# Moving the half-width set to place two, and the seven-product sets to places 3, 5 and 6

## The chip, the core and the metric

The kernel runs on one core of a Trainium2 chip. The metric is the device time of one launch in microseconds (us). TensorE does the matmuls (PE in the profile, with its weight loads as PEld), VectorE is DVE, ScalarE is ACT, GpSimd is POOL, and SyncE (SP) issues most transfers from HBM. Each of these engines works through its own instructions strictly in the order in which the built program has them, and waits where an operand is not there yet.

## The reference

A decoder trunk of four layers on 256 tokens of width 1024, all in float32. Each layer is: half a step of a SwiGLU feed-forward net, a token mixer, and half a step of a second feed-forward net. So there are eight feed-forward nets (FFNs), and the change touches only these:

```
def swiglu_ffn(x, w_gate_up, w_down):            # w_gate_up 1024 x 5632, w_down 2816 x 1024
    gate, up = jnp.split(x @ w_gate_up, 2, axis=-1)
    return (jax.nn.silu(gate) * up) @ w_down

x = x + 0.5 * rms_norm(swiglu_ffn(rms_norm(x, g[0]), ffn_w_gate_up[i, 0], ffn_w_down[i, 0]), g[1])
...                                              # the mixer
x = x + 0.5 * rms_norm(swiglu_ffn(rms_norm(x, g[4]), ffn_w_gate_up[i, 1], ffn_w_down[i, 1]), g[5])
```

## The kernel before, in words

**Precision.** Every float32 operand is split into a rounded part `hi` (written by ACT, L312) and the rest `lo` (written by DVE, L313). A product is three matmuls: hi·hi, hi·lo, lo·hi. Weights come from HBM as tiles of 128x1024 (512 KB), called units here. A unit is loaded into one of 5 `raw` buffers, split into one of 10 `hi`/`lo` buffer pairs (the ring, `RING = 10`), and used by PE. `pump` splits units ahead of their use, in the order of one list (`plan`), up to nine units ahead of the one that PE has finished with; `slot` is called after each unit, says that its buffers are free, issues one outstanding quad load and splits up to two units.

**An FFN.** The 2816 columns of the inner width are 22 blocks of 128. They are worked in six sets, each at a place in the order: `WIDTH` gives the blocks of each, five with 4 and one with 2. A full set makes 512 gate and 512 up columns for two tiles of 128 tokens. There are three ways to do a set:

- *The first set* and the one at place 5 are plain: eight units (g0 to g3, u0 to u3), each with 12 matmuls of 128x512.
- *The half-width set* (`e`, two blocks) puts 256 gate and 256 up columns in one tile: four units of 12 matmuls.
- *The seven-product sets* (function `seven`, the places in `SEVEN`) treat the set as a 2x2 block product (two token tiles, two halves of the 1024 inputs, gate and up columns) and do it with seven block products instead of eight. Each product (operations 0 to 6) is two split units of 6 matmuls, 84 matmuls in all against 96. The price is on the other engines. The weights come as four *quads* (tiles of 128x2x1024, two halves each, eight loads of 512 KB on SP), held in buffers that all FFNs share (`mgh`, `mgl`, `rows`) and one of the FFN's own (`q22`). They are added to each other in place: `gather` on POOL's queue adds one quad to another by DMA (L271, halves 0 and 1 of the fourth quad onto the second, later the sum onto the third), and DVE adds in place ahead of operation 2 (L285) and subtracts ahead of operation 4 (L288). All 14 splits then read the quads, so a split can wait for a gather. On the output side ACT copies an accumulator aside while PE goes on (`snap`, L632: after operations 0, 2 and 3), and DVE combines copies and accumulators (L644 after operation 1, L655 after 4, L661 after 5, L666 and L667 after 6).

**Down units.** One unit D of the down projection (12 matmuls for both token tiles) can be used once its block has been transposed. `FILL` says how many D units follow each part of a set; the last eight of the 22 are held back and done first for token tile 0, then for tile 1, so that the norm of tile 0 runs beside the second pass. A finished set is transposed (`turned`, L565 on PE, then splits on ACT and DVE) in the middle of the next one, the last set after the second of the eight held units.

**What sets the order.** The Python order of the calls fixes which unit is split and loaded when; a scheduler then places instructions on each engine's queue. PE, DVE, ACT, POOL and SP then run their queues in that order.

**Quad loads before.** `new_quad` makes the eight loads of a set outstanding. It is called at the start of the FFN for the set at place 2, and at the start of the set ahead for those at places 4 and 6.

Of the kernel before, what the change touches and what calls it, by code (L numbers as in the profile page):

```python
# [52 lines left out]
N_OUT = {0: 8, 1: 4, 2: 8}  # L53


WIDTH = (4, 4, 2, 4, 4, 4)
SETS = len(WIDTH)
FIRST = tuple(sum(WIDTH[:s]) for s in range(SETS))
SEVEN = (1, 3, 5)
FILL = {1: (2, 2), 2: (2,), 3: (2, 0), 4: (1, 1), 5: (2, 2)}  # L60
QUADS = 8


def ffn_chunks(l, f):
# [8 lines left out]
    for s in range(SETS):  # L73
        if s in SEVEN:
            for ops, n in zip(((0, 1, 2), (3, 4, 5, 6)), FILL[s]):
                order += [("S", l, f, s, op, h) for op in ops for h in range(2)]
                fill(n)
            continue
        for c, n in zip(("e",) if WIDTH[s] == 2 else ("g", "u"), FILL.get(s, (0, 0))):
            order += [(c, l, f, s, i) for i in range(4)]  # L80
# [125 lines left out]
class Trunk:  # L206
    def __init__(self, ctx, tc, io):
        self.ctx, self.tc, self.nc, self.io = ctx, tc, tc.nc, io
        pool = lambda name, bufs=1, **kw: ctx.enter_context(tc.tile_pool(name=name, bufs=bufs, **kw))
        self.const = pool("const")  # L210
        self.wp = pool("wp")
        self.main = pool("main")
        self.small = pool("small", 4)
        self.ps = pool("ps", space=bass.MemoryType.PSUM)
        self.dram = pool("dram", space=bass.MemoryType.DRAM)
        self.plan = plan()
        self.offs = {}
        o = 0
        for key in load_order():
            a, b = unit_shape(key)  # L220
            self.offs[key] = o
            o += P * a * b
        self.raw_order = [key for key in self.plan if key[0] != "S"]
        self.loaded = self.split_n = self.taken = self.released = 0
        self.raws = deque()
        self.ready = deque()
        self.bg = deque()
        self.xf = {}
        self.quad = None
        self.quad_loads = deque()  # L230

    def rot(self, *shape):
        t = self.ps.tile([P, 512], F32, tag="rot", name="rot", bufs=4)
# [17 lines left out]
        self.raws.append((t, a * b))  # L251
        self.loaded += 1

    def new_quad(self, fp, l, f, s):
        self.quad = [None] * 4
        self.quad_pool = fp
        self.quad_set = (l, f, s)
        self.quad_loads = deque(quads(l, f, s))

# [31 lines left out]
    def split_next(self):  # L291
        key = self.plan[self.split_n]
        hi = self.wp.tile([P, 1024], F32R, tag="hi", name="hi", bufs=RING)
        lo = self.wp.tile([P, 1024], F32R, tag="lo", name="lo", bufs=RING)
        if key[0] == "S":
            for _ in range(self.quads_for(key)):
                self.load_quad()
            self.split(hi, lo, self.operand(*key[4:]))
        else:
            t, n = self.raws.popleft()  # L300
            self.split(hi[:, :n], lo[:, :n], t[:, :n])
            self.load_next()
        self.ready.append((hi, lo))
        self.split_n += 1
# [232 lines left out]
    def ffn(self, l, f, post_next, pre_next, last=False):  # L537
        nc, tc = self.nc, self.tc
        with tc.tile_pool(name=f"ffn{l}{f}", bufs=1, reuse_waits="tile") as fp:
# [16 lines left out]
            def turn_set(s, t):  # L556
                if t == 0:
                    if WIDTH[s] == 2:
                        hs[s] = tuple(fp.tile([P, 2, SEQ], F32R, tag=n, name=n) for n in ("eh", "el"))
                    else:  # L560
                        hs[s] = tuple(fp.tile([P, 4, SEQ], F32R, tag=n, name=n, bufs=2) for n in ("hh", "hl"))
                n = WIDTH[s]
                ps = self.rot()
# [7 lines left out]
            def first_set():  # L571
                T[0] = [tile_T(), tile_T()]
                held = [self.take("g", l, f, 0, i) for i in range(4)]
                for t in range(2):
                    g = self.rot()
                    for i in range(4):
                        pair(held[i], g, i, t)
                        self.slot(t)
                    silu(T[0][t], g)
                    u = self.rot()  # L580
                    if t == 0:
                        held.extend(self.take("u", l, f, 0, i) for i in range(4))
                    for i in range(4):
                        pair(held[4 + i], u, i, t)
                        self.slot(t)
                        if t == 0 and i == 2:
                            self.trans(1, keep=self.keep)
                    nc.vector.tensor_tensor(out=T[0][t], in0=T[0][t], in1=u, op=ALU.mult)
# [80 lines left out]
                product(s, 6, c, False, c12)  # L669
                fill(FILL[s][1])  # L670

            self.new_quad(fp, l, f, 1)
            first_set()
            left = sums()
            gn = {"pre": None}
# [36 lines left out]

            for s in range(1, SETS):
                T[s] = [tile_T(), tile_T()]
                if s + 1 in SEVEN:
                    self.new_quad(fp, l, f, s + 1)
                if s in SEVEN:
                    seven(s)
                    if s == max(SEVEN):
                        self.bg.append(gains)  # L720
                    if s == max(SEVEN) and (l, f) == (0, 0):
                        self.bg.extend(self.setup2())
# [5 lines left out]
                after = lambda s=s: turned(s - 1)  # L728
                if WIDTH[s] == 2:
                    ps = half("e", s, after, 2)  # L730
# [617 lines left out]
```

## Time and profile before

| | |
|---|---|
| runs, median (lowest to highest of 3) | 1889.15 us (1886.43 to 1889.77) |
| the profiled execution, its own time | 1888.2 us |
| its span | 1886.4 us |
| PE, DVE, ACT, POOL busy | 98%, 81%, 60%, 8% of the span |
| granted TensorE clock, mean | 0.996 |
| splits: from raw tiles, from quads | 451 and 336 on ACT, as many on DVE |
| gathers on POOL | 96, twelve to an FFN |

The profiled execution is 0.95 us under the median. A matmul is shown as 0.39 us though the next one starts 0.227 us after it: they are pipelined, and PE's busy share says little about waits. Waits on PE are read from the idle time with its releaser, and from distances between starts.

### The profile page before, as it was taken

Reading aid. Unit: us, or ns where it says so; the run is one execution under the profiler, and the core shown is the slowest. Engines: PE = TensorE matmul, PEld = TensorE weight load, DVE = VectorE, ACT = ScalarE, POOL = GpSimd, SP = SyncE. Lnnn points to the kernel's source line nnn. Section 1 sums busy time; section 2 is a strip of 40 time slices with the busy share of each in tenths; the row PEclk is TensorE's granted clock in tenths of the full one; section 3 lists DMA queues with packets and bytes.
Section 4 is the critical chain, followed back from the end, with each engine's and each line's share of the span. In section 5 each row is a group of like instructions: output and inputs, shape, how many; then the busy total and the mean of one; then the engine's idle time right before and its main releaser. Section 6 shows DMA issues by size and latency. Waiting matters only on the chain.

```text
span 1886.4 us, 25346 instructions
## 1 busy us (share of the span) xinstructions
PE 1842.0 (98%) x9310; PEld 1535.2 (81%) x9310; DVE 1537.1 (81%) x1868; ACT 1132.7 (60%) x1541; POOL 150.2 (8%) x211
## 2 busy tenths in 40 slices
PE   7999999999999999999999999999999999999998
PEld 5788887878788797778878889877788888987886
DVE  6888878987988768888789876879887988879884
ACT  5666656656665655656666666556665666656652
POOL 0000201000100100100010000010001000201000
PEclk9999999999999999999999999999999999999999
DMA  8886748776786662677668667358775786738862
GB/s 295 257 265 225 224 136 264 227 243 223 226 261 194 235 220 101 201 242 247 215 210 263 211 218 257 105 190 256 247 245 169 245 264 204 247 125 273 256 192 78
DMA packets 117692, 413.01 MB, mean 219 GB/s; under 512 B 13620, under 2 KB 18112, under 8 KB 117440
## 3 DMA queue, kind: packets, MB, share of 16 engines
q1 hardware_dynamic: 103568, 359.47, 54.2%
q0 software_dynamic: 14000, 51.92, 13.8%
q8 instruction: 73, 1.20, 0.3%
q14 instruction: 51, 0.42, 0.1%
HBM read 359.95 MB, written 1.06 MB: 191 GB/s over the span
## 4 chain that ended last, share of the span: by engine, by line
PE 41%; DVE 7%; DMA 3%; issue 2%; ACT 1%; POOL 1%; DVEq 0%; ACTq 0%; POOLq 0%
PE acc L696 12%; PE rot L624 9%; PE rot L337 5%; PE rot L339 5%; PE rot L338 5%; DVE lo L313 5%; PE acc L960 2%; DMA quad<-quad 2%; DMA quad<-in_w 1%; PE rot L565 1%; PE acc L880 1%; DVE quad L288 1%; PE rot L894 1%; PE rot L862 1%; ACT hi L312 0%
## 5 line engine op out<-in xcount | busy, mean ns | idle before, releaser
L313 DVE TENSOR_TENSOR lo<-raw,hi 128x1024 fp32r<-128x1024 f32 (+2 forms) x451 | 536.3, 1217 | 77.6 <-ACT hi L312 74.7
L312 ACT ACTIVATE hi<-raw 128x1024 fp32r<-128x1024 f32 (+2 forms) x451 | 463.2, 1051 | 198.3 <-DMA raw<-in_w 96.7
L312 ACT ACTIVATE hi<-quad 128x1024 fp32r<-128x1024 f32 x336 | 343.6, 1053 | 227.5 <-DVE quad L285 131.8
L313 DVE TENSOR_TENSOR lo<-quad,hi 128x1024 fp32r<-128x1024 f32 x336 | 397.5, 1219 | 20.7 <-ACT hi L312 19.9
L339 PE MATMUL rot<-hi,xtl 128*128 128x512 f32 (+3 forms) x816 | 312.8, 384 | 3.9 <-DVE xtl L313 3.9
L337 PE MATMUL rot<-hi,xth 128*128 128x512 f32 (+3 forms) x816 | 315.0, 386 | 0.4 <-ACT hi L312 0.4
L338 PE MATMUL rot<-lo,xth 128*128 128x512 f32 (+3 forms) x816 | 312.0, 382 | 0.3 <-DVE lo L313 0.3
L624 PE MATMUL rot<-hi,sums 128*128 128x512 f32 x768 | 255.1, 398 | 16.2 <-ACT snap L632 8.0
L696 PE MATMUL acc<-hi,hh 128*128 128x512 f32 x640 | 199.4, 391 | 0.0
L696 PE MATMUL acc<-lo,hh 128*128 128x512 f32 x640 | 198.9, 390 | 0.0
L696 PE MATMUL acc<-hi,hl 128*128 128x512 f32 x640 | 197.9, 390 | 0.0
L624 PEld LDWEIGHTS rot<-hi,sums 128*128 128x128 f32 x768 | 145.8, 190 | 52.9 <-ACT snap L632 12.3
L339 PEld LDWEIGHTS rot<-hi,xtl 128*128 128x128 f32 x816 | 153.7, 188 | 37.0 <-DVE xtl L313 8.3
L337 PEld LDWEIGHTS rot<-hi,xth 128*128 128x128 f32 x816 | 153.8, 189 | 29.2 <-ACT hi L312 1.0
L338 PEld LDWEIGHTS rot<-lo,xth 128*128 128x128 f32 x816 | 153.8, 188 | 29.2 <-DVE lo L313 0.5
L624 PE MATMUL rot<-lo,sums 128*128 128x512 f32 x384 | 151.2, 394 | 2.1 <-DVE lo L313 2.1
L271 POOL DMA_DIRECT2D quad<-quad x96 | 83.7, 897 | 837.6 <-DMA quad<-in_w 394.5
L696 PEld LDWEIGHTS acc<-hi,hl 128*128 128x128 f32 x640 | 119.6, 188 | 26.9 <-DVE hl L313 2.2
L696 PEld LDWEIGHTS acc<-lo,hh 128*128 128x128 f32 x640 | 119.9, 188 | 24.7
L696 PEld LDWEIGHTS acc<-hi,hh 128*128 128x128 f32 x640 | 119.7, 188 | 24.5
L624 PE MATMUL rot<-hi,xtl 128*128 128x512 f32 x288 | 112.1, 389 | 0.0
L624 PE MATMUL rot<-hi,xth 128*128 128x512 f32 x288 | 112.0, 389 | 0.0
(214 smaller groups left out, 2571.3 us busy)
## 6 DMA issues: line engine op xcount, KB each, us to landing
raw<-in_w SPq DMA_DIRECT2D x440, 512.0 KB, 4.8
quad<-in_w SPq DMA_DIRECT2D x192, 512.0 KB, 5.1
quad<-quad POOLq DMA_DIRECT2D x96, 512.0 KB, 4.7
gpre<-in_norm_g SPq DMA_DIRECT2D x8, 512.0 KB, 6.3
gpost<-in_norm_g SPq DMA_DIRECT2D x8, 512.0 KB, 3.4
memraw<-in_mem_t SPq DMA_DIRECT2D x32, 128.0 KB, 3.6
g<-in_norm_g SPq DMA_DIRECT2D x8, 512.0 KB, 6.7
raw<-in_w SPq DMA_DIRECT2D x8, 384.0 KB, 4.1
```

The costliest lines, as they stand in the source:

```text
L271: self.nc.gpsimd.dma_start(out=x, in_=y, accum_op=ALU.add)
L288: self.nc.vector.tensor_tensor(out=b11, in0=b11, in1=b22, op=ALU.subtract)
L312: self.nc.scalar.activation(out=hi, in_=src, func=AF.Copy)
L313: self.nc.vector.tensor_tensor(out=lo, in0=src, in1=hi.bitcast(F32), op=ALU.subtract)
L337: mm(out, a[0], b[0], start=start, stop=False)
L338: mm(out, a[0], b[1], start=False, stop=False)
L339: mm(out, a[1], b[0], start=False, stop=stop)
L565: nc.tensor.transpose(ps[:, k * P:(k + 1) * P], T[s][t][:, k * P:(k + 1) * P], self.ident)
L624: nc.tensor.matmul(ps, a[i], w[j][:, kk, :], start=fresh and h == kk == i == j == 0, stop=h == kk == i == 1, skip_group_check=True)
L696: mm(ys[t][:, n * 512:(n + 1) * 512], x, y[:, 0, n * 512:(n + 1) * 512], start=(j == 0 and x is a[0] and y is w[0]), stop=(j == NF - 1 and ...
L862: nc.tensor.transpose(ps[:, i * P:(i + 1) * P], blocks[b0 + i], self.ident)
L960: self.nc.tensor.matmul(o["y"][t][:, h * 512:(h + 1) * 512], x, y[:, 0, h * 512:(h + 1) * 512], start=(j == 0 and x is a[0] and y is w[0]) ...
```

## The change

Three tables and the time at which quad loads are made outstanding are changed. The half-width set goes from place 3 to place 2. The seven-product sets go from places 2, 4 and 6 to places 3, 5 and 6, and the plain set from place 5 to place 4, so that the last two sets are both seven-product sets and stand next to each other. The same units, matmuls and bytes are left; their order differs, and with it which columns belong to which set.

The D units between are dealt out anew. Fourteen are done ahead of the eight held ones, as before. A seven-product set had two in its middle (after operation 2) and now has one; six now stand between the seven-product sets at places 5 and 6, and none stands between the last product of place 6 and the held units, where there were two.

The quad loads of a set are now made outstanding in `split_next`, right after the second half of operation 6 of the seven-product set ahead is split (`new_quad` takes the next from `quad_wait`), and for the first of an FFN at the first set's up units, four slots later than before.

```
-WIDTH = (4, 4, 2, 4, 4, 4)
+WIDTH = (4, 2, 4, 4, 4, 4)
...
-SEVEN = (1, 3, 5)
-FILL = {1: (2, 2), 2: (2,), 3: (2, 0), 4: (1, 1), 5: (2, 2)}
+SEVEN = (2, 4, 5)
+FILL = {1: (2,), 2: (1, 1), 3: (1, 1), 4: (1, 6), 5: (1, 0)}
...
+        self.quad_wait = deque()
...
-    def new_quad(self, fp, l, f, s):
+    def new_quad(self):
+        self.quad = None
+        if not self.quad_wait:
+            return
+        self.quad_pool, l, f, s = self.quad_wait.popleft()
         self.quad = [None] * 4
-        self.quad_pool = fp
         self.quad_set = (l, f, s)
         self.quad_loads = deque(quads(l, f, s))
...
             self.split(hi, lo, self.operand(*key[4:]))
+            if key[4:] == (6, 1):
+                self.new_quad()
...
                     if t == 0:
+                        self.quad_wait.extend((fp, l, f, s) for s in SEVEN)
+                        self.new_quad()
                         held.extend(self.take("u", l, f, 0, i) for i in range(4))
...
-            self.new_quad(fp, l, f, 1)
             first_set()
...
-                if s + 1 in SEVEN:
-                    self.new_quad(fp, l, f, s + 1)
                 if s in SEVEN:
                     seven(s)
```

In the changed file the lines stand a little lower: the split is L318 and L319, the gather L275, the additions L289 and L292, the transposes L571, the products L632, the copy aside L640, the combinations L652, L663, L669, L674 and L675, and the D units L703.

**Gathers on POOL, layer 1, first FFN.** Each seven-product set has four: two add the fourth quad to the second, two add the sum that DVE makes of it to the third, and the last two cannot start before DVE has read what the first two made. Before, in the order of places 2, 4 and 6:

```order
L271 DMA quad_4298<-quad_4313 128x1024 x2
L271 DMA quad_4280<-quad_4261 128x1024 x2
L271 DMA quad_4808<-quad_4833 128x1024
L271 DMA quad_4751<-quad_4716 128x1024
L271 DMA quad_4808<-quad_4833 128x1024
L271 DMA quad_4751<-quad_4716 128x1024
L271 DMA quad_5188<-quad_5221 128x1024 x2
L271 DMA quad_5133<-quad_5096 128x1024 x2
```

Now, in the order of places 3, 5 and 6:

```order
L275 DMA quad_4344<-quad_4371 128x1024 x2
L275 DMA quad_4309<-quad_4294 128x1024 x2
L275 DMA quad_4741<-quad_4771 128x1024 x2
L275 DMA quad_4712<-quad_4683 128x1024 x2
L275 DMA quad_5181<-quad_5211 128x1024 x2
L275 DMA quad_5152<-quad_5123 128x1024 x2
```

At place 4 the second gather of the first kind stood behind a gather of the second kind. No set has that any more; it was so in six of the eight FFNs (all but the two of layer 0).

**PE at the end of the last set, layer 1, first FFN.** L624 is the last matmul of operation 6, `acc` the sum of the down projection, L565 the transposes of the last set's two token tiles. Before (the last row of operation 6 and ten of the 18 rows of D units; eight more follow, the last six of them of the first two held units, and then the transposes):

```order
L624 MATMUL rot_5441<-hi_5393,sums_4449 128x512
L696 MATMUL acc_4452<-hi_5409,hh_5139 128x512 x2
L696 MATMUL acc_4452<-lo_5410,hh_5139 128x512 x2
L696 MATMUL acc_4452<-hi_5409,hl_5140 128x512 x2
L696 MATMUL acc_4453<-hi_5409,hh_5139 128x512 x2
L696 MATMUL acc_4453<-lo_5410,hh_5139 128x512 x2
L696 MATMUL acc_4453<-hi_5409,hl_5140 128x512 x2
L696 MATMUL acc_4452<-hi_5421,hh_5139 128x512 x2
L696 MATMUL acc_4452<-lo_5422,hh_5139 128x512 x2
L696 MATMUL acc_4452<-hi_5421,hl_5140 128x512 x2
L696 MATMUL acc_4453<-hi_5421,hh_5139 128x512 x2
```

Now:

```order
L632 MATMUL rot_5477<-hi_5429,sums_4453 128x512
L703 MATMUL acc_4456<-hi_5445,hh_5395 128x512 x2
L703 MATMUL acc_4456<-lo_5446,hh_5395 128x512 x2
L703 MATMUL acc_4456<-hi_5445,hl_5396 128x512 x2
L703 MATMUL acc_4456<-hi_5457,hh_5395 128x512 x2
L703 MATMUL acc_4456<-lo_5458,hh_5395 128x512 x2
L703 MATMUL acc_4456<-hi_5457,hl_5396 128x512 x2
L703 MATMUL acc_4456<-hi_5471,hh_5395 128x512 x2
L703 MATMUL acc_4456<-lo_5472,hh_5395 128x512 x2
L571 MATMUL rot_5580<-ident_74,T_5344 128x128 x4
L571 MATMUL rot_5587<-ident_74,T_5345 128x128 x4
```

Between operation 6 and the transposes stood 36 matmuls (18 rows of two), and now stand 16. In the very last FFN it is 12.

**DVE at the same place.** From the split of operation 6's second half (from a quad) to the product that the transposes read (L667 before, L675 now), before:

```order
L313 TENSOR_TENSOR lo_5462<-raw_5272,hi_5461 128x1024
L655 TENSOR_TENSOR snap_5433<-rot_5441,snap_5433 128x512
L313 TENSOR_TENSOR lo_5474<-raw_5413,hi_5473 128x1024
L313 TENSOR_TENSOR lo_5489<-raw_5425,hi_5488 128x1024
L546 SCALAR_TENSOR_TENSOR T_5293<-T_5293,rot_5294 128x512
L313 TENSOR_TENSOR lo_5501<-raw_5439,hi_5500 128x1024
L661 TENSOR_TENSOR T_5293<-T_5293,snap_5433 128x512
L666 TENSOR_TENSOR snap_5375<-rot_5441,snap_5375 128x512
L313 TENSOR_TENSOR lo_5515<-raw_5452,hi_5514 128x1024
L667 TENSOR_TENSOR T_5292<-T_5292,snap_5375 128x512
```

Now:

```order
L319 TENSOR_TENSOR lo_5498<-raw_5310,hi_5497 128x1024
L663 TENSOR_TENSOR snap_5469<-rot_5477,snap_5469 128x512
L319 TENSOR_TENSOR lo_5510<-raw_5449,hi_5509 128x1024
L319 TENSOR_TENSOR lo_5525<-raw_5461,hi_5524 128x1024
L552 SCALAR_TENSOR_TENSOR T_5345<-T_5345,rot_5346 128x512
L319 TENSOR_TENSOR lo_5537<-raw_5475,hi_5536 128x1024
L669 TENSOR_TENSOR T_5345<-T_5345,snap_5469 128x512
L674 TENSOR_TENSOR snap_5427<-rot_5477,snap_5427 128x512
L319 TENSOR_TENSOR lo_5551<-raw_5488,hi_5550 128x1024
L675 TENSOR_TENSOR T_5344<-T_5344,snap_5427 128x512
```

In both, four more splits from raw tiles stand between that of operation 6 and the first row shown. The queue of DVE up to the product is as long as before: nine splits and five combinations.

## The prediction

> **What bounds the kernel now.** I read the page's first part, then the waits of PE, then the stretches around single waits. Of the page:
>
> ```profile
> span 1886.4 us, 25346 instructions
> PE 1842.0 (98%) x9310; PEld 1535.2 (81%) x9310; DVE 1537.1 (81%) x1868; ACT 1132.7 (60%) x1541; POOL 150.2 (8%) x211
> ```
>
> PE is the bound, and the change leaves its matmuls as they are. So only PE's waits can be gained or lost. The chain of waits gives the pace without a wait:
>
> ```profile
> 1393.39 10.88 PE rot L624 x48
> 1404.27 8.16 PE acc L696 x36
> ```
>
> That is 10.88 / 48 = 0.227 us a matmul; 6 of one split unit take 1.36 us, 12 of a D unit 2.72. Of the waits of PE (total, times, longest) these five rows belong to seven-product sets:
>
> ```profile
> PE rot L624 <- ACT snap L632: 8.0, 10, 1.6
> PE rot L624 <- DVE snap L655: 4.7, 5, 2.6
> PE rot L624 <- ACT hi L312: 3.4, 1, 3.4
> PE rot L624 <- DVE lo L313: 2.1, 1, 2.1
> PE rot L565 <- DVE T L588: 1.5, 1, 1.5
> ```
>
> 19.7 us in 18 waits. A matmul is shown as 0.39 us and the next could start after 0.227, so each wait is 0.16 longer than its row: 2.9 more, 22.6.
>
> Where are they? One FFN (layer 2, second), by stretch: place 2, place 4, place 6 (columns: length, then busy time of PE, PEld, DVE, ACT, POOL, then clock share, DMA share and GB/s).
>
> ```profile
> 1272.00:1304.00 32.00, 29.32 (x132) 23.74 (x131) 30.36 (x33) 22.79 (x28) 2.57 (x3) 1.00 0.80 245
> 1318.00:1351.00 33.00, 31.24 (x139) 25.34 (x138) 27.88 (x30) 20.89 (x26) 1.72 (x2) 1.00 0.76 232
> 1378.00:1404.00 26.00, 26.00 (x120) 21.61 (x120) 25.12 (x27) 19.02 (x22) 0.00 (x0) 1.00 0.72 238
> ```
>
> PE idles 2.7 us at place 2, 1.8 at place 4 and nothing at place 6. DVE is nearly full in all three; what place 6 has is a plain set ahead of it.
>
> **The waits cost clock too.** Two of them in the timeline (start, length, instruction, idle time ahead and what ended it), and the stretches around them (the column behind POOL is the clock share):
>
> ```profile
> 46.23 0.51 PE L624 MATMUL rot<-hi,sums 128*128 128x512 f32 x1 [3.40 <-ACT hi L312]
> 386.54 0.80 PE L624 MATMUL rot<-hi,sums 128*128 128x512 f32 x1 [2.62 <-DVE snap L655]
> ```
>
> ```profile
> 48.00:52.00 4.00, 3.20 (x8) 2.53 (x9) 4.00 (x5) 4.00 (x5) 0.87 (x1) 0.51 1.07 212
> 52.00:56.00 4.00, 4.00 (x13) 3.17 (x12) 4.00 (x4) 1.09 (x2) 0.00 (x0) 0.64 0.69 225
> 384.00:388.00 4.00, 1.46 (x4) 1.17 (x5) 3.64 (x5) 2.17 (x3) 0.00 (x0) 0.75 0.91 286
> 388.00:392.00 4.00, 4.00 (x16) 3.25 (x15) 3.88 (x5) 2.92 (x4) 0.00 (x0) 0.83 1.00 387
> ```
>
> Missing share times length: 4 x (0.49 + 0.36) = 3.4 us behind the first, 4 x (0.25 + 0.17) = 1.7 behind the second. With these 5.1 the waits of the seven-product sets come to **27.7 us**.
>
> [...]
>
> **What makes a wait at place 4,** in the same FFN:
>
> ```profile
> 1314.09 0.86 POOL L271 DMA_DIRECT2D quad<-quad  x1 [12.62 <-DVE quad L285]
> 1315.23 0.85 POOL L271 DMA_DIRECT2D quad<-quad  x1 [0.28 <-DMA quad<-in_w]
> 1322.77 1.23 DVE L285 TENSOR_TENSOR quad<-quad 128x1024 f32<-128x1024 f32 x1 [2.59 <-DMA quad<-quad]
> 1324.09 1.06 ACT L312 ACTIVATE hi<-quad 128x1024 fp32r<-128x1024 f32 x1 [5.59 <-DVE quad L285]
> 1329.79 0.57 ACT L632 ACTIVATE snap<-rot 128x512 f32<-128x512 f32 x1
> 1330.41 0.50 PE L624 MATMUL rot<-hi,sums 128*128 128x512 f32 x1 [1.02 <-ACT snap L632]
> ```
>
> POOL holds the second gather of the fourth quad behind a gather that waits for DVE (12.62 us); it lands 7.5 us after its issue; DVE's addition waits for it; ACT, in order, waits 5.6 us for the addition, and the copy aside (`snap`), queued behind it, comes 1.0 us too late for PE.
>
> **The change part by part.**
>
> *Place 4 to place 5 (gathers in order, a plain set ahead).* The build pairs the gathers in every set, so the 12.62 us wait has no place left on POOL, and the order of place 5 is that of the old place 6: a plain set, then seven products. That row had no PE wait. Differences: one D unit in the middle instead of two, so PE goes through 2.72 us faster there and DVE has one split (about 1.13) less to do: 1.6 us of lead lost.
>
> *Place 2 to place 3 (half-width set between).* Ahead of place 2, DVE had no slack:
>
> ```profile
> 493.00:536.00 43.00, 42.68 (x192) 34.80 (x191) 40.95 (x43) 28.27 (x33) 2.83 (x4) 1.00 0.83 265
> 30.00:40.00 10.00, 10.00 (x46) 8.27 (x45) 7.37 (x9) 5.86 (x7) 0.81 (x1) 1.00 0.90 359
> ```
>
> ```profile
> 39.19 1.97 POOL L271 DMA_DIRECT2D quad<-quad  x2 [23.14 <-DMA quad<-in_w]
> ```
>
> 41 us busy of 43 (first set and place 2 of a later FFN); and in the very first FFN the gathers started only at 39.2. Now four `e` units and two D units stand between: 48 + 24 matmuls, 16.3 us of PE, for six splits, 6.8 us of DVE, and the copies and combinations fall 16.3 us later than the first set's sums. The first FFN's loads get four raw units ahead of or among them, 2.1 MB, some 6 us at the 359 GB/s of the start; 10 us of the 16.3 remain against waits of 3.4 and 2.1. So all of place 2's waits should go, the half clock of the first FFN with them.
>
> *Place 6.* It follows a seven-product set, which drains DVE's lead, but six D units stand between: 16.3 us of PE against 6.8 of splits and five combinations of 0.6: 6.5 us of lead regained, more than the 1.6 lost. The quad loads start at the split of the last operation ahead of it, nine units before PE gets there; its last half-load still stands behind six raw loads, as at the old place 6 it stood behind some, and the slack to operation 2 is over 20 us of PE work. I cost the loads at nothing; if that cover is gone, the wait is one gather's, 5 to 7.5 us per FFN.
>
> What is left for the three places: 0 by place 6's row, (1.02 + 0.74) x 8 = 14 by place 4's two waits (the second is the combination after operation 4, L655, in that FFN). I take 2, near place 6, since the structure is that of place 6.
>
> *The end of the last set.* This is the added cost. Its transposes need the product L667, which needs operation 6. When operation 6 ended (the first D matmul) and when the product started, in three FFNs:
>
> ```profile
> 171.67 0.61 PE L696 MATMUL acc<-hi,hh 128*128 128x512 f32 x2
> 176.34 0.68 DVE L667 TENSOR_TENSOR T<-T,snap 128x512 f32<-128x512 f32 x1
> 1404.11 0.61 PE L696 MATMUL acc<-hi,hh 128*128 128x512 f32 x2
> 1406.67 1.22 DVE L313 TENSOR_TENSOR lo<-raw,hi 128x1024 fp32r<-128x1024 f32 x1 [0.78 <-ACT hi L312]
> 1407.81 0.68 DVE L667 TENSOR_TENSOR T<-T,snap 128x512 f32<-128x512 f32 x1
> 1850.37 0.62 PE L696 MATMUL acc<-hi,hh 128*128 128x512 f32 x2
> 1853.20 0.68 DVE L667 TENSOR_TENSOR T<-T,snap 128x512 f32<-128x512 f32 x1
> ```
>
> The lag to the product's end is 5.35, 4.38 and 3.51 us, mean 4.4. It was covered by 36 matmuls, 8.16 us. Now 16 cover 3.63 us, and DVE's queue up to the product is as long as before. So PE waits about 0.8 us in each of seven FFNs: 5.5. In the last one the queue is a split shorter, and its 3.51 - 1.13 = 2.4 us fit under 12 matmuls (2.72). The lead lost (up to 1.6 us) can add 7 x 1.6 = 11. Bounds 0 (if all lags were as the last) and 17; I take 8, near the rows. Behind the waiting transposes stand the rest of the first token tile's D units, and behind those the norm: a wait there goes straight into the end.
>
> *Nothing for:* the later start of the first quad loads (four slots, 5.4 us, of the 16.3 gained), the position tables of layer 0 (they ride on the seven-product set and move with it), the same bytes and splits.
>
> **Sum.** 27.7 gained, 2 left over, 8 new: 17.7. 1888.2 - 17.7 = 1870.5 for a profiled execution; the median of the runs stood 0.95 above it, so 1871.5 us.
>
> **Rivals.**
>
> *The waits move with the sets.* The copy aside is still queued on ACT behind splits that need DVE's additions. For it: ten of the 18 waits are of this kind. Against it: place 6 has the same queue and none. If place 3 keeps the waits of place 2 outside the first FFN (the 8.0 less some 2 for place 4, which had 1.02 in the FFN shown; the 1.5 of L588; 0.16 each for ten: 9.1), the time is 1880.6. Chance 0.17.
>
> *DVE does not recover between the neighbours: slower.* The combination after operation 4 must be done before operation 6 starts, and five splits stand ahead of it on DVE: 5 x 1.13 + 0.68 + 1.36 = 7.7 us of lead needed at the last split of operation 6. Place 6 had this:
>
> ```profile
> 1389.77 3.49 DVE L313 TENSOR_TENSOR lo<-quad,hi 128x1024 fp32r<-128x1024 f32 x3
> ```
>
> split done at 1393.26, its half of operation 6 started 1.36 before 1404.11, at 1402.75: 9.5 us. Less 1.6 leaves 7.9, a margin of 0.2. Every microsecond below 7.7 is a PE wait in each FFN; at 4 it is 3.7 x 8 = 30 and the time 1902. It decides from a lead of 5.1 (2.6 x 8 = 21, the gain and 0.2% with it). For it: the margin. Against: the six D units, and that the lead of the old place 6 was set by waiting for PE, not by DVE's speed. Chance 0.10.
>
> *The start hides nothing:* the loads are begun earlier, but what limits a set is the landing of the last half quad, still behind raw loads in SP's order, so no wait goes: 1889. For it: that half did come late at place 4. Against: the pairing. Chance 0.08.
>
> *The end of the last set is free:* lags under 3.6 us everywhere as in the last FFN, and no leftovers: 1861.5. Chance 0.10.
>
> **How the numbers follow.** The forecast has 0.55, its own range 1863 to 1879. With the rival at 1880.6, the free end at 1861.5 and half of what lies around them, 1859 to 1887 holds 8 in 10; the bounds of the terms (27.7 - 14 - 17) would reach 1892. A difference under 0.2% (3.8 us) can't be told from none here. Faster: 0.55 + 0.10 + most of 0.17 = 0.81; the same: 0.08 and a little = 0.09; slower 0.10.
>
> **What would show it.** Right: no PE wait for the copy aside or for L588's successor; clock share 1.00 from 40 us on; a new wait of the transposes (L571) for the product L675, about 1 us, in seven FFNs. Wrong: PE waits for the combination after operation 4 at place 6 (lead), additions on DVE that wait for a gather at place 5 or 6 and a PE wait behind them (loads), or waits in the first set, which I took as unchanged.

## The result, and the profile after

The changed kernel takes 1916.29 us (median of 4 runs, 1911.38 to 1921.96) against 1889.02 us for the kernel before in the same comparison: a ratio of 1.0148, 95% interval 1.0114 to 1.0181. It is slower by some 27 us. The forecast was 1871.5, with a range of 1859 to 1887 and a chance of 0.10 for slower.

The page of the changed kernel (its profiled execution took 1911.38 us):

```profile
span 1909.6 us, 25374 instructions
PE 1847.3 (97%) x9310; PEld 1536.9 (80%) x9310; DVE 1538.7 (81%) x1868; ACT 1139.8 (60%) x1541; POOL 149.7 (8%) x211
```

The profile is of the fastest of the four runs. The work is the same to the instruction on PE and DVE; the span is 23.2 us longer. The waits of PE (total, times, longest):

```profile
PE rot L409 <- DVE rows L395: 15.8, 9, 8.4
PE rot L343 <- DVE hl L319: 13.0, 8, 2.6
PE rot L571 <- DVE T L675: 10.7, 8, 1.9
PE acc L703 <- ACT hh L318: 3.9, 3, 1.8
PE rot L632 <- ACT snap L640: 3.4, 3, 2.2
PE rot L490 <- DVE memf L488: 2.7, 1, 2.7
```

The waits of the seven-product sets have shrunk from 18 waits, 19.7 us, to 3 waits of 3.4 us (L632). That half of the forecast came true. Above that row stand rows that the kernel before did not have. The two largest are L343, the first `u` unit of the plain set at place 4, which waits for the splits `hl` of transposes, and L571, the transposes of the last set. (`hh`, made by ACT, and `hl`, made by DVE from it, are the two parts of a transposed set.)

Distances between the starts of PE's matmuls, less the pace of 0.227 us, give the whole account (half clock behind a wait counted with it: behind the wait that ended at 852.93 the granted clock is 0.50 in each microsecond from 854 to 857, and the matmuls start 0.43 us apart):

| us of PE above the pace | before | after |
|---|---|---|
| seven-product sets | 28.3 | 4.1 |
| plain set at place 4: wait before u0 (8), half clock behind four of them | 0 | 14.3 + 7.0 |
| half-width set at place 2 and the D units behind it (three FFNs) | 0 | 8.5 |
| transposes of the last set (8) | 0 | 12.0 |
| end of an FFN: the norm (L409), and L490 in the first FFN | 0.8 | 9.5 |

So 24.2 us were recovered, 50.5 came in, and 3.1 were regained elsewhere, which I did not follow.

Why does u0 wait at place 4? DVE in layer 2, first FFN (start, length, instruction, idle time ahead and what ended it):

```profile
1028.32 1.23 DVE L289 TENSOR_TENSOR quad<-quad 128x1024 f32<-128x1024 f32 x1
1029.46 1.22 DVE L319 TENSOR_TENSOR lo<-quad,hi 128x1024 fp32r<-128x1024 f32 x1
1034.52 1.23 DVE L289 TENSOR_TENSOR quad<-quad 128x1024 f32<-128x1024 f32 x1 [3.85 <-DMA quad<-quad]
1035.67 1.22 DVE L319 TENSOR_TENSOR lo<-quad,hi 128x1024 fp32r<-128x1024 f32 x1
1036.80 1.28 DVE L319 TENSOR_TENSOR hl<-rot,hh 128x512 fp32r<-128x512 f32 x2
```

The additions and `lo<-quad` splits belong to the next set, place 5; the `hl` splits read the accumulators of place 3's transposes. PE transposed at 1029.26 and ACT made `hh` from 1030.42 to 1031.49; DVE stood idle from 1030.68 and could have made `hl` then. But the second addition stands ahead, and it waits for a gather. It is so in seven of the eight FFNs; in the very first, `hl` stands behind the first addition only, which waits 5.98 us there. PE:

```profile
1035.14 0.61 PE L703 MATMUL acc<-hi,el 128*128 128x512 f32 x2
1037.54 0.50 PE L343 MATMUL rot<-hi,xth 128*128 128x512 f32 x1 [1.78 <-DVE hl L319]
```

u0 needs two of the four `rot` accumulators; `g` holds two and the unread transposes the other two. Now the same place in the kernel before (plain set at place 5, additions of place 6), same FFN:

```profile
1054.35 1.22 DVE L285 TENSOR_TENSOR quad<-quad 128x1024 f32<-128x1024 f32 x1
1055.49 2.35 DVE L313 TENSOR_TENSOR lo<-quad,hi 128x1024 fp32r<-128x1024 f32 x2
1057.76 1.28 DVE L313 TENSOR_TENSOR hl<-rot,hh 128x512 fp32r<-128x512 f32 x2
1058.96 1.27 DVE L546 SCALAR_TENSOR_TENSOR T<-T,rot 128x512 f32<-128x512 f32 x2
1060.15 1.22 DVE L313 TENSOR_TENSOR lo<-quad,hi 128x1024 fp32r<-128x1024 f32 x1
1064.42 1.23 DVE L285 TENSOR_TENSOR quad<-quad 128x1024 f32<-128x1024 f32 x1 [3.05 <-DMA quad<-quad]
```

There the addition waits as well, 3.05 us, but the `hl` splits stand ahead of it and nobody notices. The places look alike in the source; the queue does not.

The additions of both kernels as a group (busy, mean ns, idle time ahead and what ended it), before and after:

```profile
L285 DVE TENSOR_TENSOR quad<-quad 128x1024 f32<-128x1024 f32 x48 | 58.7, 1224 | 44.4 <-DMA quad<-quad 44.1
```

```profile
L289 DVE TENSOR_TENSOR quad<-quad 128x1024 f32<-128x1024 f32 x48 | 58.3, 1221 | 88.5 <-DMA quad<-quad 88.3
```

DVE's time in waiting for gathers has doubled. The gather waits in its turn for the second half of the fourth quad: that half load was issued at 1018.33, its neighbour, the first half, at 1007.20 (the last of the five in the first row). Seven raw loads stand between them on SP (SP's rows, and POOL's of the gather):

```profile
1000.08 7.44 SPq L243 DMA_DIRECT2D quad<-in_w  x5
1008.28 10.00 SPq L243 DMA_DIRECT2D raw<-in_w  x7
1018.33 0.42 SPq L243 DMA_DIRECT2D quad<-in_w  x1
1026.30 0.86 POOL L275 DMA_DIRECT2D quad<-quad  x1 [14.47 <-DMA quad<-in_w]
```

The half landed at 1025.78, the gather that POOL then issued at 1034.43.

In the half-width set the queue is ACT's. In the three FFNs that lose time there, `hh` of the first set's transposes stands on ACT behind splits of quads that wait for place 3's additions on DVE. In layer 2's second FFN ACT is idle 2.23 us for the second addition, which waits 2.06 us for its gather; `hh` comes next, and the D units wait 0.62 us for it.

### The profile page after: what moved, and what is told of

Its sections match the earlier page's. It is cut to its first block, busy times and chain, and to the rows that moved or that the text cites. A ratio compares the mean times of both kernels' runs of the same rounds, so it can differ in the third digit from the quotient of the medians.

```text
span 1909.6 us, 25374 instructions
## 1 busy us (share of the span) xinstructions
PE 1847.3 (97%) x9310; PEld 1536.9 (80%) x9310; DVE 1538.7 (81%) x1868; ACT 1139.8 (60%) x1541; POOL 149.7 (8%) x211
## 4 chain that ended last, share of the span: by engine, by line
PE 58%; DMA 14%; DVE 11%; issue 8%; ACT 3%; POOL 1%; SPq 1%; ACTq 0%; DVEq 0%; POOLq 0%
PE rot L632 15%; PE acc L703 15%; PE rot L343 7%; PE rot L345 7%; PE rot L344 7%; DVE lo L319 7%; DMA quad<-quad 4%; DMA quad<-in_w 4%; DMA raw<-in_w 3%; PE acc L965 3%; ACT hi L318 2%; DMA memraw<-in_mem_t 1%; PE rot L571 1%; PE rot L867 1%; PE rot L899 1%
## 5 line engine op out<-in xcount | busy, mean ns | idle before, releaser
L319 DVE TENSOR_TENSOR lo<-raw,hi 128x1024 fp32r<-128x1024 f32 (+2 forms) x451 | 539.4, 1218 | 71.5 <-ACT hi L318 68.4
L318 ACT ACTIVATE hi<-raw 128x1024 fp32r<-128x1024 f32 (+2 forms) x451 | 466.6, 1051 | 175.9 <-DMA raw<-in_w 67.8
L318 ACT ACTIVATE hi<-quad 128x1024 fp32r<-128x1024 f32 x336 | 349.2, 1057 | 280.5 <-DVE quad L289 112.3
L319 DVE TENSOR_TENSOR lo<-quad,hi 128x1024 fp32r<-128x1024 f32 x336 | 401.5, 1218 | 27.6 <-ACT hi L318 24.8
L343 PE MATMUL rot<-hi,xth 128*128 128x512 f32 (+3 forms) x816 | 318.3, 390 | 13.4 <-DVE hl L319 13.0
L632 PE MATMUL rot<-hi,sums 128*128 128x512 f32 x768 | 251.6, 394 | 3.5 <-ACT snap L640 3.4
L703 PE MATMUL acc<-hi,hh 128*128 128x512 f32 x640 | 198.3, 391 | 3.9 <-ACT hh L318 3.9
L703 PE MATMUL acc<-hi,hl 128*128 128x512 f32 x640 | 199.1, 392 | 0.9 <-DVE hl L319 0.9
L703 PE MATMUL acc<-lo,hh 128*128 128x512 f32 x640 | 198.5, 391 | 0.0
L343 PEld LDWEIGHTS rot<-hi,xth 128*128 128x128 f32 x816 | 155.5, 191 | 46.0 <-DVE hl L319 16.4
L632 PEld LDWEIGHTS rot<-hi,sums 128*128 128x128 f32 x768 | 144.2, 188 | 36.1 <-ACT snap L640 5.8
L275 POOL DMA_DIRECT2D quad<-quad x96 | 83.5, 891 | 929.5 <-DMA quad<-in_w 543.8
L632 PE MATMUL rot<-lo,sums 128*128 128x512 f32 x384 | 149.6, 390 | 0.0
L703 PEld LDWEIGHTS acc<-hi,hh 128*128 128x128 f32 x640 | 120.4, 189 | 30.2 <-ACT hh L318 5.1
L703 PEld LDWEIGHTS acc<-hi,hl 128*128 128x128 f32 x640 | 119.6, 188 | 26.6 <-DVE hl L319 2.2
L703 PEld LDWEIGHTS acc<-lo,hh 128*128 128x128 f32 x640 | 120.0, 188 | 24.8
L289 DVE TENSOR_TENSOR quad<-quad 128x1024 f32<-128x1024 f32 x48 | 58.3, 1221 | 88.5 <-DMA quad<-quad 88.3
L632 PE MATMUL rot<-hi,xtl 128*128 128x512 f32 x288 | 112.1, 389 | 0.0
```

What stands on the lines that cost most here:

```text
L275: self.nc.gpsimd.dma_start(out=x, in_=y, accum_op=ALU.add)
L289: self.nc.vector.tensor_tensor(out=b11, in0=b11, in1=b12, op=ALU.add)
L318: self.nc.scalar.activation(out=hi, in_=src, func=AF.Copy)
L319: self.nc.vector.tensor_tensor(out=lo, in0=src, in1=hi.bitcast(F32), op=ALU.subtract)
L343: mm(out, a[0], b[0], start=start, stop=False)
L632: nc.tensor.matmul(ps, a[i], w[j][:, kk, :], start=fresh and h == kk == i == j == 0, stop=h == kk == i == 1, skip_group_check=True)
```

## The experiments

The theory, **T**: with the loads begun earlier, the build places both additions ahead of `hl`; the second one waits for a gather whose half load is late; PE waits for `hl`. **R1**: DVE is simply behind, since it has no lead between or after seven-product sets. **R2**: PE's cover at the end of the last set is too short, whatever the loads do. All ratios are against the kernel before, timed on the same chip.

### Loads of place 5 begun later (late5)

```
-            if key[4:] == (6, 1):
+            if key[4:] == (6, 1) and key[3] == 4:
                 self.new_quad()
...
             for s in range(1, SETS):
                 T[s] = [tile_T(), tile_T()]
+                if s == 3:
+                    self.new_quad()
```

> Against the changed kernel, only the quad loads of the set at place 5 are begun later: at the start of the plain set at place 4 (as the kernel before did for its last set), not at the last split of place 3. The theory: in the changed kernel the early loads let the build place both DVE additions of place 5 (L289) ahead of the splits (hl) of the transposes that stand in the plain set; the second addition waits for a gather, the transposes' accumulators are not read, and PE waits before u0 (13.0 us in 8 waits, with the stretches around them and the half clock behind them 21). In this kernel seven of the eight FFNs have the hl splits between the two additions and one ahead of both. So the theory expects L343 <- DVE hl under 3 us, no half clock at place 4, and about 21 us less than the changed kernel: 1895 us (1890 to 1900). First rival, that what counts is when the fourth quad lands: it now lands later, so the second addition comes later and PE waits more, 3 to 8 us in each FFN: 1940 to 1980. Second rival, that DVE is simply behind at place 4 after the seven-product set: the waits stay, 1911 to 1920.

1901.14 us, ratio 1.0068 (1.0045 to 1.0092): 15 us less than the changed kernel, against some 21 expected. The row L343 <- DVE hl is gone, and the mean granted clock of the profiled execution is 0.996, against 0.994 in the changed kernel. But the additions of place 5 now wait longer (38.6 us in all, against 32.9), and PE's waits for copies aside (L632), 3.4 us in the changed kernel, are 6.4 in 6 waits. A *later* load start is faster here: that fits T alone. The rival by which only the landing counts expected 1940 and more.

### Transposes one unit earlier (at1)

```
-                ps = half("g", s, after, 2)
+                ps = half("g", s, after, 1)
```

> Against the changed kernel, the transposes in the plain set at place 4 stand after g1 and not after g2, 12 matmuls (2.72 us) earlier; loads are as in the changed kernel. The build then places the hl splits ahead of the second addition of place 5 in all FFNs. The theory (hl queued on DVE behind an addition that waits for a gather) expects the same gain as from the later loads: L343 <- DVE hl under 3 us and 1890 to 1900 us, unless the transposes now wait for their product (L675 ended 4.4 us ahead of the transposes in one FFN, so 1.7 is left: nothing to 3 us in all). If DVE were simply behind, the 2.72 us would be the most that an FFN can gain, and the waits of DVE's later work would come out elsewhere: 1905 to 1916.

1894.08 us, ratio 1.0032 (1.0021 to 1.0043): 22 us less, what the waits before u0 and their half clock came to (21.3). The same place, with the loads untouched:

```profile
1017.69 1.23 DVE L289 TENSOR_TENSOR quad<-quad 128x1024 f32<-128x1024 f32 x1
1018.84 1.22 DVE L319 TENSOR_TENSOR lo<-quad,hi 128x1024 fp32r<-128x1024 f32 x1
1019.97 1.28 DVE L319 TENSOR_TENSOR hl<-rot,hh 128x512 fp32r<-128x512 f32 x2
1025.52 1.22 DVE L289 TENSOR_TENSOR quad<-quad 128x1024 f32<-128x1024 f32 x1 [4.27 <-DMA quad<-quad]
```

The addition still waits, 4.27 us here, now behind the `hl` splits, and PE has no wait for them. R1 expected at most 11 us.

### Two D units back at the end of the last set (tail)

```
-FILL = {1: (2,), 2: (1, 1), 3: (1, 1), 4: (1, 6), 5: (1, 0)}
+FILL = {1: (2,), 2: (1, 1), 3: (1, 1), 4: (1, 4), 5: (1, 2)}
```

> Against the changed kernel, two of the six D units between places 5 and 6 go back to the end of the last set, so that 40 matmuls (9.1 us) and not 16 (3.6 us) stand between operation 6 and the transposes of the last set. The theory (cover: the product L675 ends 5 to 6 us after operation 6) expects all eight waits L571 <- DVE T L675 to go, 12.0 us with the 0.16 of each, and perhaps the 3.0 us wait in the very first FFN's end: 1901 to 1904. If those two units were needed as lead between the neighbouring sets, the copies and combinations of place 6 get waits of PE: each microsecond of lead missing costs 8 us, and the time stays at 1911 to 1920.

1937.25 us, ratio 1.0253 (1.0228 to 1.0279): a clear miss. The waits at the end of the last set are gone, but place 6 has new ones (eight of the ten in the first row, 24.3 us). Behind the longest of them, 4.52 us, which ended at 1418.87, the matmuls start 0.43 us apart and not 0.227; the mean granted clock is 0.985 against 0.994 in the changed kernel:

```profile
PE rot L632 <- ACT snap L640: 26.9, 10, 4.5
PE rot L343 <- DVE hl L319: 17.2, 8, 3.4
```

So the six D units between the neighbours were needed. Whether as lead for DVE (R1) or as cover for a late gather, this run doesn't tell: at place 6 too the second addition waits, here the longest of eight:

```profile
1407.82 1.22 DVE L289 TENSOR_TENSOR quad<-quad 128x1024 f32<-128x1024 f32 x1 [7.04 <-DMA quad<-quad]
```

### The earlier loads alone, in the old order (before_early)

The kernel before, with `new_quad` moved to the last split of the seven-product set ahead, as in the change, and nothing else:

> The kernel before with one part of the change alone: its places and D units are kept, and the quad loads are begun as in the changed kernel (at the last split of the seven-product set ahead; for the first of an FFN as before, at its start). The build then places both additions of the last set ahead of the plain set's hl splits in six of eight FFNs, as in the changed kernel. The theory expects waits of PE for DVE hl at place 5 in those six FFNs, 1.3 to 2.7 us each with half clock behind some: 8 to 18 us more there. What the gathers at place 4 do is open (its own waits were 5 of the 28 us): 1894 to 1907 us. If the neighbouring of the sets or the place of the half-width set were to blame for the waits at place 4, this kernel would have none of them and come out at 1884 to 1891.

1922.08 us, ratio 1.0173 (1.0145 to 1.0200), 33 us slower than the kernel before. The direction is T's, the size (1894 to 1907) is not: besides the row that T expected (16.6 us), the D units behind the half-width set, which there stands between places 2 and 4, wait for *their* `hl` behind place 4's additions.

```profile
PE rot L343 <- DVE hl L319: 16.6, 6, 3.5
PE acc L703 <- DVE hl L319: 10.7, 7, 2.1
```

The load start by itself costs as much as the whole change. Neither the neighbouring of the sets nor the place of the half-width set is needed for the loss.

### Two quad loads in a slot (two_loads)

```
-        if self.quad_loads:
+        for _ in range(min(2, len(self.quad_loads))):
             self.load_quad()
```

> Against the changed kernel, a slot issues two outstanding quad loads and not one. The build then has the last half load of the set at place 5 four raw loads further ahead on SP, and of place 6 three; DVE's order at place 4 is the same, both additions ahead of the hl splits. The raw loads there are 1.1 to 1.8 us apart, so the half should land 5 to 6 us earlier, and the second addition, which waited 3.9 us for its gather in one FFN, should not wait. If the hl splits are late because the addition ahead of them waits for the gather, the 13.0 us of L343 <- DVE hl fall under 4 and the half clock behind them goes: 1893 to 1902 us. If the place in the queue alone matters, or DVE is behind, the time stays at 1911 to 1920.

1875.75 us, ratio 0.9937 (0.9919 to 0.9956): 40 us less than the changed kernel, twice what I expected, and faster than the kernel before. Place 4 again, DVE's order as in the changed kernel:

```profile
1011.53 1.23 DVE L289 TENSOR_TENSOR quad<-quad 128x1024 f32<-128x1024 f32 x1
1012.67 1.22 DVE L319 TENSOR_TENSOR lo<-quad,hi 128x1024 fp32r<-128x1024 f32 x1
1013.92 1.23 DVE L289 TENSOR_TENSOR quad<-quad 128x1024 f32<-128x1024 f32 x1
1015.07 1.22 DVE L319 TENSOR_TENSOR lo<-quad,hi 128x1024 fp32r<-128x1024 f32 x1
1016.20 1.28 DVE L319 TENSOR_TENSOR hl<-rot,hh 128x512 fp32r<-128x512 f32 x2
```

Same queue, no wait; three raw loads, not seven, stand between the two halves here. The order and the late load each are necessary; taking away either one ends the stall. And the row that I had laid to short cover shrank tenfold, with the D units where the change put them:

```profile
PE rot L571 <- DVE T L675: 1.1, 3, 0.6
```

In layer 2's second FFN the last product ended 4.95 us after operation 6 in the changed kernel (1421.90 to 1426.85) and 3.52 here (1394.64 to 1398.16), against 3.6 us of cover. At place 6 the second addition had waited 5.58 us there and waits 2.57 here. DVE came late to the end of the last set because it had stood still for a gather earlier in that set. So R2, which has the loads not matter, falls; the short cover is needed for the wait all the same, since in `tail`, with 36 matmuls of cover, it was gone too.

### Both cures, and the D units again (at1_two, at1_two_tail, at1_two_e1)

Transposes after g1 and two loads in a slot; then with four D units between places 5 and 6; then with five, and the transposes of the half-width set after its second unit:

> Transposes after g1 (1894.1 us alone) and two quad loads in a slot. Both cures are for the same wait at place 4, so nothing more is to be had there: 1888 to 1895. What could come on top is the half-width set, where the splits of the first set's transposes stand behind place 3's additions in the second FFN of each layer (8.5 us in three FFNs): their gathers should land earlier.

> As the kernel before this, and two D units from between places 5 and 6 back to the end of the last set. With four D units between and one load in a slot, PE waited 27 us at place 6 for the copy aside (L640) and DVE's second addition waited 7.0 us for a gather whose half quad came late. If that late half is the cause, three raw loads earlier (4 to 5 us) should take most of these waits away, and the end of the last set gives its 12 us: 1876 to 1886. If DVE lacks the lead between neighbouring seven-product sets, whatever the loads do, the waits at place 6 stay near 27 us and the time is 1905 to 1920.

> Transposes after g1, two quad loads in a slot, one D unit (not two) moved from between places 5 and 6 to the end of the last set, and the transposes in the half-width set after its second unit, so that 24 matmuls (5.4 us) and not 12 cover the splits of the first set's transposes. At the end of the last set 28 matmuls cover 6.35 us against lags of 5 to 6: the waits there should fall from 10.7 to under 2. In the half-width set the 8.5 us should go, unless the transposes now wait for the first set's product. Theory: 1872 to 1880. If neither cover helps, 1888 to 1895.

1878.10 us (ratio 0.9946, 0.9927 to 0.9966), 1895.97 (1.0053, 1.0037 to 1.0068) and 1876.09 (0.9941, 0.9919 to 0.9963). The cures don't add up, as expected: they cure one wait; 1878 is below the 1888 to 1895 that I gave, since I had priced two loads without the end of the last set. In the third kernel the waits at the end of the last set are gone and the half-width set's too, but others came in their place, 6.7 us of them in the first FFN alone. With four D units PE still waited for the copy aside at place 6:

```profile
PE rot L632 <- ACT snap L640: 14.5, 13, 2.2
```

That is 14.5 us against 24.3. Both readings had missed: 1876 to 1886 by the late half, and 1905 to 1920 by the lead.

### Four D units, and no gather at place 6 (four_no_gather)

The second of the three kernels above; in addition the gathers of the fourth quad at place 6 are left out, a part of the computation (16 of the 96 gathers) that its time does not contain; every DVE instruction is there:

```
-        if q == 3:
+        if q == 3 and key[3] != 5:
             self.gather(...)
```

> Transposes after g1, two loads in a slot, four D units between places 5 and 6 (1896.0 us as such, with 14.5 us of PE's waits for the copy aside at place 6 and half clock behind some of them), and with the gathers of the fourth quad at place 6 left out, a part of the computation. DVE's instructions are all there; only the additions wait for no gather. If the late half load was what PE waited for at place 6, the waits go and with them the half clock, and the time is 1874 to 1882. If DVE lacks the lead between neighbouring sets, with four D units between (10.9 us of PE against 4.5 of splits and 3 of combinations), most of the waits stay: 1888 to 1896.

1867.49 us, ratio 0.9891 (0.9876 to 0.9905), below the 1874 to 1882 expected. No wait for a copy aside is left at all. With the same splits, combinations and D units, in the same order on DVE, the waits went with the gather. So four D units are lead enough for DVE's own work, and R1 as it stands falls: at place 6 it is the wait for the gather that needs more lead, and six D units cover it (two_loads and at1_two have no such wait). The run also takes the gathers' traffic away; how much of the gain that is, no run separates.

### Two loads in the kernel before (before_two)

The same edit as in two_loads, on the kernel before:

> The kernel before, with two quad loads in a slot and nothing else changed. It tells what the change of places is worth once the loads come in time: the changed kernel with two loads came to 1875.8 us. In the kernel before, the second additions of its last set wait 1.9 to 3.6 us for gathers, but the hl splits stand ahead of them and PE waits for neither; its own waits (place 2, and the gather at place 4 that POOL holds behind another one) do not hang on the last half load alone. If the change of places recovers the waits of the seven-product sets, as forecast, this kernel stays within 8 us of the kernel before, 1880 to 1889. If the two loads are all that counts and the places are worth nothing, it comes to 1874 to 1878 as well.

1887.80 us, ratio 0.9997 (0.9984 to 1.0010). Alone it is worth nothing. So the change as a whole is worth about 11 us once two loads go out in a slot (0.9937 against 0.9997), and costs 27 with one. The 27 are not the price of the places: the earlier start alone, in the old places, cost 33 (1.0173 against 1.0148 for the whole change, with intervals that overlap).

### Four loads in a slot, and the first loads earlier (four_loads, two_first)

> The changed kernel with four quad loads in a slot. The last half load stands behind one raw load at places 5 and 6, against three at two loads and seven and six at one. The second additions at place 6, which waited 5.0 to 6.4 us at one load and 2.6 to 3.9 at two, should wait 0 to 2. PE had nothing left to gain there at two loads but the 1.1 us at the end of the last set: 1872 to 1876. If the quad loads now hold up the raw loads behind them, splits come late and the time rises, 1878 to 1885.

> The changed kernel with two quad loads in a slot, and the first loads of an FFN begun at its start as in the kernel before (not at the up units). In the very first FFN of the kernel with two loads the first addition waits 5.2 us for its gather and PE loses 5.3 us behind it, half clock included; in two later FFNs the half-width set loses 2.3 us. These should go: 1868 to 1873. Against it: the first raw loads of the program come later, where PE already waits 5 us in the first 18 us: if so, 1874 to 1879.

1887.06 us (ratio 0.9998, 0.9984 to 1.0012; above both ranges that I gave) and 1877.22 (0.9946, 0.9931 to 0.9961). With four loads the additions wait less, 20.9 us in all against 39.1 at two, but the raw units wait more; ACT's splits of raw units wait 99.8 us for their loads against 69.2 at two (the group's idle time, first four loads, then two):

```profile
L318 ACT ACTIVATE hi<-raw 128x1024 fp32r<-128x1024 f32 (+2 forms) x451 | 468.2, 1052 | 222.2 <-DMA raw<-in_w 99.8 <-issue 46.3 <-PE rot L345 30.2
```

```profile
L318 ACT ACTIVATE hi<-raw 128x1024 fp32r<-128x1024 f32 (+2 forms) x451 | 468.3, 1052 | 198.8 <-DMA raw<-in_w 69.2 <-issue 42.7 <-PE rot L345 30.0
```

and L343 <- DVE hl is back with 11.4 us: DVE reaches `hl` late because the splits ahead of it came late. In layer 2's first FFN three of its splits of raw tiles waited 3.04, 0.68 and 0.76 us for ACT's there, and those 3.20, 0.96 and 2.13 us for their loads. Earlier first loads gained nothing: the first addition of the first FFN waits 4.7 us instead of 5.2, and the first 18 us of the program are as they were. My expectation there was wrong, and why that gather lands no earlier I did not find out.

Idle time of DVE ahead of the 48 additions, by set, with PE's two rows and the time:

| kernel | 1st set | 2nd | 3rd | L343 <- hl | L571 <- T | us |
|---|---|---|---|---|---|---|
| before | 9.9 | 8.4 | 26.1 | none | none | 1889 |
| changed | 10.6 | 32.9 | 45.0 | 13.0 | 10.7 | 1916 |
| at1 | 11.0 | 25.1 | 43.7 | none | 10.3 | 1894 |
| two_loads | 11.8 | 0.4 | 26.9 | none | 1.1 | 1876 |
| four_loads | 11.4 | 0.4 | 9.1 | 11.4 | 0.3 | 1887 |
| before_early | 9.9 | 23.8 | 26.4 | 16.6 | none | 1922 |
| before_two | 8.9 | 11.2 | 20.0 | 0.3 | none | 1888 |

(Where the places are the old ones, the row of L571, there also under the name L565, has a wait of 1.2 to 1.5 us that belongs to place 2; it is left out.)

## Why the prediction was wrong

**The seven-product waits: right.** 27.7 us were to be had and 2 left over; 28.3 were there and 4.1 are left. The pairing of the gathers and the half-width set ahead of place 3 together did what the prediction said; no run separates the two.

**"I cost the loads at nothing": this step failed.** The prediction did see that the last half load stands behind six raw loads, and that its price, cover gone, is one gather, "5 to 7.5 us per FFN". It set this aside because PE had over 20 us of work left. That slack was reckoned to operation 2's matmuls. The first to suffer was not operation 2 but whatever else stands behind the addition on DVE: at place 4 the splits of another set's transposes, whose buffers the next PE unit needs; at place 6 the last products of the set. Counted in DVE's queue there was no slack: the waits of DVE for gathers rose from 44.1 to 88.3 us, and PE lost 21.3 us before u0, which went with the late load (two_loads) or with the order (at1).

**"The order of place 5 is that of the old place 6": wrong in the one row that mattered.** At the old place 6 `hl` stood between the two additions, and now behind both. The kernels late5 and before_early show that the load start itself moves it: earlier loads let the build put the additions further forward. The prediction compared POOL's order and the end of the last set, and not DVE's order around the transposes of the plain set. Its cost is 21.3 us there. Another 8.5 came in at the half-width set, where on ACT `hh` stands behind splits that wait for place 3's additions.

**The end of the last set: right sign and right path, 12.0 against 8.** The cover shrank as the prediction said. The lag from the end of operation 6 to the end of the product hardly changed: in the first seven FFNs it is 4.8 us on average in the kernel before and 5.0 in the changed one. The 4.4 of the sum was the mean of three lags, and one of them was the short one of the last FFN, which the sum treats on its own. What the prediction didn't see is where the lag comes from. It took it as given by the length of the queue; but in four_no_gather, with the same splits and combinations, it is 3.5 to 3.6 us in all eight FFNs. The rest is made earlier at place 6, where DVE stands still for the gather. With two loads the cover is as short and 1.1 us of wait is left. (In at1_two, also with two loads, the first two FFNs keep lags of 5.1 and 5.3; why, I did not find out.)

**The rivals.** "DVE does not recover between neighbours" named the right side, 1902 and slower, but the wrong mechanism: without place 6's gather even four D units are enough, and with it six are. "The start hides nothing" had the right mechanism, the last half behind raw loads, and priced it as no change: it took for granted that a wait that is not removed costs what it did before. With one sentence more (where does DVE stand while it waits?) it would have been the rival on the other side.

**Half clock.** The prediction counted it behind waits of 3.40 and 2.62 us. Four of the eight new waits at place 4 (those of 1.78, 1.87, 2.01 and 2.58 us) were followed by it too, 1.74 us each: the granted clock was 0.57, 0.60, 0.57 and 0.57 over 4 us from 1038, 853, 1345 and 99. Behind the other four (0.51, 0.91, 1.47 and 1.87 us) it was 1.00 over 4 us from 1802, 378, 1529 and 561. The sum had no term for this.

**Not in the prediction:** 8.7 us more at the ends of FFNs. The norm's waits stay with two loads (row L409, in which some 8 us belong to the program's start: 15.0 us in 8 waits, against 15.8 in 9 in the changed kernel) and are smaller in four_no_gather, where two D units stand at the last set's end again (11.8 in 7); L490, 2.7 to 4.0 us in the first FFN, stays in all kernels with the new places. What exactly makes these late was not tried.

**What would have been right:** with loads in time the change gains 12 us against the 17.7 of the sum. The version with two loads in a slot, 1875.75 us, beats both kernels.

## What to carry to other kernels

An engine that waited for a transfer held up here what stood behind the wait in its queue, not only the transfer's own reader: in layer 2's first FFN DVE stood 3.85 us for a gather, and PE waited 1.78 us for the `hl` splits behind that addition. So the slack of a load has to be read in the queue of the engine that waits, row by row, up to the first instruction that someone else needs. Starting loads earlier is not harmless by itself: here it changed the order that the build chose and moved additions that wait for gathers ahead of the `hl` splits (1922 us in before_early, against 1889). Between too late and too dense lies a setting to be measured: one, two and four loads in a slot gave 1916, 1876 and 1887 us.

## What the runs showed of the hardware

The length of an idle time alone did not decide here whether the clock fell. In the changed kernel PE stood idle 1.87 us both before 561.13 and before 852.93. Starts of u0 and the granted clock (behind POOL) around each:

```profile
561.13 0.50 PE L343 MATMUL rot<-hi,xth 128*128 128x512 f32 x1 [1.87 <-DVE hl L319]
852.93 0.50 PE L343 MATMUL rot<-hi,xth 128*128 128x512 f32 x1 [1.87 <-DVE hl L319]
```

```profile
562.00:566.00 4.00, 4.00 (x19) 3.32 (x18) 3.13 (x4) 1.06 (x1) 0.87 (x1) 1.00 0.74 146
854.00:858.00 4.00, 4.00 (x12) 3.14 (x11) 3.87 (x5) 0.38 (x1) 0.86 (x1) 0.60 0.83 164
```

After the first the clock stayed full, after the second it was 0.60 over those 4 us, with 0.50 in each microsecond from 854 to 857; an idle time of 1.44 us (ahead of 329.65; another of 0.38 followed it) was followed by a share of 0.70 from 330 to 334, and one of 2.24 (ahead of 1628.97) by 1.00 from 1630 to 1634. So 1.87 us were followed by a fall once and not the other time, and 2.24 us by none; what else decides it, no run shows.
